# One decoder layer on one core: TensorE's feed at the start and at the two phase borders rearranged

## The chip, the cores and the metric

The kernel runs on one core of one Trainium2 chip. The metric is the device time of one execution in microseconds, as the median of several runs. The core's engines are TensorE (PE, matrix products; its weight loads are listed as PEld), VectorE (DVE), ScalarE (ACT), GpSimd (POOL) and SyncE (SP, which only issues transfers here). They run in parallel and wait for each other by semaphores.

## The reference, cut to what matters

One step of a decoder trunk with one layer, for 256 prompt tokens and 8 x 4 sample tokens (288 columns in all), model width 2048, feed-forward width 5632, all in float32:

```python
x = x + 0.5 * rmsnorm(swiglu(rmsnorm(x, g[0]), ffn1_w_in, ffn1_w_out), g[1])
m, sg, sh = hybrid_mixer(rmsnorm(x, g[2]), mix_w_in, ..., mix_w_out, s_gla, s_hgrn)
x = x + rmsnorm(m, g[3])
x = x + 0.5 * rmsnorm(swiglu(rmsnorm(x, g[4]), ffn2_w_in, ffn2_w_out), g[5])
```

`swiglu` is `(silu(gate) * up) @ w_out` with `gate, up` from `x @ w_in`. `hybrid_mixer` projects to queries, keys, values and gates, runs two groups of gated linear recurrences (GLA: 4 heads of 128 x 256 state; HGRN2: 8 heads of 128 x 128), each from a given state for the sample tokens, normalises the heads and projects back with `mix_w_out`. The outputs are the tokens and the new states.

## The kernel before

**Layout.** Model columns lie on the partitions, tokens along the free axis: `x[k]`, k = 0 to 15, are 16 tiles of 128 x 288. A float32 product is made of three products in the faster `fp32r` type: every weight `w` is split into `wh` (rounded, by ACT, L101) and `wl = w - wh` (by DVE, L102), and every `x` tile into `xh` (ACT, L272) and `xl` (DVE, L273). L556 to L558 are then `xh wh`, `xl wh` and `xh wl`, 128 x 288 results summed up in PSUM. So each tile of 128 x 128 weights costs PE three matmuls.

**Weights.** Class `Weights` (L40) moves all weights in units of 128 x 1024 (512 KB): `load` issues the transfer of a unit on SP's queue into one of three `raw` buffers, `pieces` splits it into one of four `wh`/`wl` pairs (two more pairs, the `extra` pool, exist around the phase borders). `ahead(most)` splits further units as long as `room()` finds a pair; `W.behind` may hold instructions behind which the next splits have to be issued (L111).

**Blocks.** `block` (L547) makes 512 output columns (four PSUM tiles) from the 16 x tiles: 8 units, two x tiles (k) each, for every k the four tiles f; after each unit it calls `W.ahead`. The last unit is taken tile by tile, each followed by its evacuation. `tick(k)` runs side work after a k. Five PSUM buffers serve the blocks.

**Phases.** Phase 1 is the first feed-forward net, phase 2 the mixer, phase 3 the second net. In each the first block (`gate1_0`, `qk0`, `gate2_0`) starts while the x tiles are still being made, and its results are used unnormalised; the second block (`up1_0`, `v0`, `up2_0`) carries the squares of x (`PreNorm.tick1`, L460), summed up in `acc`; `rstd` (L441) turns `acc` by an all-ones product on PE (`pre`, L445) into `rt`, which evacuations from then on multiply by.

**Borders.** `post_norm` (L521) ends a phase: `go` and `PreNorm.tick0` call `update(k)` for the 16 tiles (on DVE `y` times the norm, L529, and `x`, L530; then `xh` on ACT and `xl` on DVE). `Fill` lets PE begin the next phase with products of the old `x` (`old`) and of the unnormalised `y` (`new`) for four tiles. At the second border the code is the same.

**Start.** Transfers of x, gains and the first weights are issued from SP and ACT (L297 and after). x comes by token and is turned on PE (`x_turn`, L317). `WARM` transposes of the identity run ahead on PE. `row` (L560) makes the first three k in an order of its own; `second` (L358) turns and splits the second tile inside the first `row`.

**Side work on POOL.** `setup` (L893 and after, run from `pn.late`) fills masks and small operands of the mixer, `a32` (L911) among them. `load_state` of `block_scan` (L1293) loads the recurrent states of the first GLA heads (256 KB each, eight buffers), L1298.

**Order.** A planner orders each engine's instructions by a model of their times, in the order of the code where nothing else decides; `tc.issue_after(ins)` puts what follows behind `ins` on `ins`'s engine. Each engine then runs its list strictly in order, so an instruction that waits holds all behind it.

## Time and profile before

| | us |
|---|---|
| median of 3 runs (2259.80 to 2262.47) | 2261.17 |
| the profiled execution, its own time | 2261.81 |
| its span, first to last instruction | 2260.0 |
| PE busy | 2248.0 (99%) |
| DVE, ACT, POOL busy | 1362.2, 1005.1, 77.9 |
| data moved | 377.94 MB, mean 167 GB/s |

Part 1 of the page gives the busy time of each engine, with matmuls counted to their modelled end, so that short halts of PE do not show there. The view of the waits, for one engine, adds up who waited for whom. The chain of waits follows the end of the program back to what released each step. The view of stretches gives the busy time of each engine in a window, with the clock granted to TensorE (1.00 is 2.4 GHz, 0.50 is 1.2 GHz) and the rate of the transfers. Timelines list instructions in order of time: start, duration, engine, line, what is written from what, and in brackets the idle time before and what ended it.

### The profile page before, as it was taken

How to read it: one execution, taken by the hardware profiler on the slowest of the kernel's cores; microseconds unless marked ns; L12 is line 12 of the kernel's file. 1: busy time of each engine (PE TensorE's matmuls, PEld its weight loads, DVE VectorE, ACT ScalarE, POOL GpSimd, SP SyncE). 2: the span in 40 equal slices, each digit the busy share in tenths (PEclk: the TensorE clock that was granted, in tenths of full speed). 3: DMA queues.
4: the chain of work that ended last, by engine and by line, in shares of the span. 5: the costliest groups of instructions: out<-in, count | busy, mean ns of one | idle time of the engine just before them, and what ended most of it. 6: DMA issues, size and time to landing. Idle time of an engine off the chain costs nothing.

```text
span 2260.0 us, 41348 instructions
## 1 busy us (share of the span) xinstructions
PE 2248.0 (99%) x17075; PEld 2230.2 (99%) x17075; DVE 1362.2 (60%) x2167; ACT 1005.1 (44%) x1509; POOL 77.9 (3%) x143
## 2 busy tenths in 40 slices
PE   9999999999999999999999999999999999999998
PEld 9999999999999999999999999999999999999998
DVE  7545545555555568778788755844555455545545
ACT  5443333333334344545565644544333343333345
POOL 0000000000000003022110000100000000000000
PEclk9999999999999999999999999999999999999999
DMA  6555555555556555476565554555555555555553
GB/s 211 168 164 165 166 168 168 163 165 168 168 163 182 169 166 163 128 217 201 172 171 166 175 184 124 168 168 166 163 167 167 168 160 167 163 166 166 167 163 115
DMA packets 207378, 377.94 MB, mean 167 GB/s; under 512 B 15426, under 2 KB 41072, under 8 KB 207184
## 3 DMA queue, kind: packets, MB, share of 16 engines
q1 hardware_dynamic: 198736, 356.56, 52.9%
q0 software_dynamic: 5984, 17.97, 2.5%
q8 instruction: 135, 2.21, 0.4%
q10 hardware_dynamic: 2464, 0.70, 0.2%
q14 instruction: 59, 0.48, 0.1%
HBM read 363.39 MB, written 11.80 MB: 166 GB/s over the span
## 4 chain that ended last, share of the span: by engine, by line
PE 96%; DVE 2%; DMA 1%; ACT 1%; issue 1%; SPq 0%; DVEq 0%; ACTq 0%
PE gate L557 10%; PE gate L558 10%; PE gate L556 10%; PE out L557 8%; PE out L558 8%; PE out L556 8%; PE up L558 8%; PE up L556 8%; PE up L557 8%; PE mo L558 2%; PE mo L556 2%; PE mo L557 1%; PE hfq L556 1%; PE hfq L557 1%; PE hfq L558 1%; PE v L556 1%
## 5 line engine op out<-in xcount | busy, mean ns | idle before, releaser
L102 DVE TENSOR_TENSOR wl<-raw,wh 128x1024 fp32r<-128x1024 f32 (+1 forms) x674 | 822.0, 1220 | 647.1 <-ACT wh L101 644.6
L101 ACT ACTIVATE wh<-raw 128x1024 fp32r<-128x1024 f32 (+1 forms) x673 | 710.6, 1057 | 1057.5 <-PE gate L557 314.0
L556 PE MATMUL gate<-xh,wh 128*128 128x288 f32 x1660 | 488.8, 298 | 0.2 <-ACT xh L272 0.2
L557 PE MATMUL gate<-xl,wh 128*128 128x288 f32 x1660 | 488.7, 296 | 0.2
L558 PE MATMUL gate<-xh,wl 128*128 128x288 f32 x1660 | 488.6, 296 | 0.0
L557 PE MATMUL out<-hl,wh 128*128 128x288 f32 x1408 | 416.4, 296 | 0.0
L556 PE MATMUL out<-hh,wh 128*128 128x288 f32 x1408 | 415.8, 295 | 0.0
L558 PE MATMUL up<-xh,wl 128*128 128x288 f32 x1408 | 415.7, 295 | 0.0
L557 PE MATMUL up<-xl,wh 128*128 128x288 f32 x1408 | 415.5, 295 | 0.0
L558 PE MATMUL out<-hh,wl 128*128 128x288 f32 x1408 | 415.5, 295 | 0.0
L556 PE MATMUL up<-xh,wh 128*128 128x288 f32 x1408 | 415.1, 295 | 0.0
L557 PEld LDWEIGHTS gate<-xl,wh 128*128 128x128 f32 x1660 | 312.0, 188 | 1.5 <-DVE xl L273 1.0
L556 PEld LDWEIGHTS gate<-xh,wh 128*128 128x128 f32 x1660 | 311.1, 189 | 1.0 <-ACT xh L272 0.7
L558 PEld LDWEIGHTS gate<-xh,wl 128*128 128x128 f32 x1660 | 312.0, 188 | 0.0
L556 PEld LDWEIGHTS out<-hh,wh 128*128 128x128 f32 x1408 | 265.1, 188 | 0.0
L558 PEld LDWEIGHTS out<-hh,wl 128*128 128x128 f32 x1408 | 265.0, 188 | 0.0
L557 PEld LDWEIGHTS out<-hl,wh 128*128 128x128 f32 x1408 | 264.9, 188 | 0.0
L558 PEld LDWEIGHTS up<-xh,wl 128*128 128x128 f32 x1408 | 264.6, 188 | 0.1
L556 PEld LDWEIGHTS up<-xh,wh 128*128 128x128 f32 x1408 | 264.4, 188 | 0.1
L557 PEld LDWEIGHTS up<-xl,wh 128*128 128x128 f32 x1408 | 264.5, 188 | 0.1
L707 DVE TENSOR_TENSOR y<-out,y 128x288 f32<-128x288 f32 x287 | 121.0, 453 | 103.3 <-PE out L558 100.5
L556 PE MATMUL hfq<-xh,wh 128*128 128x288 f32 x256 | 78.1, 305 | 0.0
(383 smaller groups left out, 2404.3 us busy)
## 6 DMA issues: line engine op xcount, KB each, us to landing
raw<-in_ffn_w_in_dram SPq DMA_DIRECT2D x351, 512.0 KB, 3.7
raw<-in_ffn_w_out_dram SPq DMA_DIRECT2D x176, 512.0 KB, 3.7
raw<-in_mix_w_in_dram SPq DMA_DIRECT2D x64, 512.0 KB, 3.7
raw<-in_mix_w_in_dram SPq DMA_DIRECT2D x96, 256.0 KB, 3.4
raw<-in_mix_w_out_dram SPq DMA_DIRECT2D x32, 512.0 KB, 3.7
out_dram<-s POOLq DMA_DIRECT2D x32, 256.0 KB, 3.4
s<-in_state_gla_dram POOLq DMA_DIRECT2D x16, 256.0 KB, 4.6
s<-in_state_hgrn_dram POOLq DMA_DIRECT2D x16, 256.0 KB, 4.5
```

The costliest lines, as they stand in the source:

```text
L101: i1 = self.nc.scalar.activation(h[:, c], raw[:, c], AF.Copy).ins
L102: i2 = self.nc.vector.tensor_tensor(l[:, c], raw[:, c], h[:, c].bitcast(F32), op=ALU.subtract).ins
L556: yield lambda: PE.matmul(dst, w[0][:, c:c + P], parts[0], start=start, stop=False)
L557: yield lambda: PE.matmul(dst, w[0][:, c:c + P], parts[1], start=False, stop=False)
L558: yield lambda: PE.matmul(dst, w[1][:, c:c + P], parts[0], start=False, stop=stop)
L707: V.tensor_tensor(y[k], ps, y[k], op=ALU.add)
```

## The change

The calls of `ahead` hold `W.behind` until a pair of buffers is free. The blank parts of the x buffers are filled ahead of the loads; the second half of the first weight unit goes to SP's queue, behind the x columns 128 to 512 of the sample tokens; the identity's transposes on PE become matmuls on a blank tile, with one among the first x transposes and four behind them, and the products `xl wh` of the first k come ahead of the second tile's transposes. `tick0` puts the next splits behind the last tile's `xh` and `xl`; `tick1` makes its squares in four ticks instead of eight and `rstd` one tick later; the sum of the fill is put ahead of the splits after the first block, which no longer splits after its unit 6. `block` gets `head`: `v0` and `up2_0` take their first two units tile by tile (f outside, k inside). On POOL a copy from `k` after the block `qk0` (`gated`) precedes the state loads and the memset of `a32`.

```diff
@@ -108,7 +108,7 @@
         return held < (2 if more else HL_BUFS)
 
     def ahead(self, most=99):
-        if self.behind is not None:
+        if self.behind is not None and self.room():
             behind, self.behind = self.behind, None
             with ExitStack() as es:
                 for ins in behind:
@@ -287,39 +287,52 @@
         nc.sync.dma_start(xins[s][:, 0:2, c0 - s * 512:c1 - s * 512],
                           x_prompt[0, :, c0:c1].rearrange("(t p) c -> p t c", p=P))
 
+    def blank_sample(c0, c1):
+        s = c0 // 512
+        V.memset(xins[s][:, 2, c0 - s * 512:c1 - s * 512], 0.0)
+
     def load_sample(c0, c1):
         s = c0 // 512
-        V.memset(xins[s][:, 2, c0 - s * 512:c1 - s * 512], 0.0)
         nc.sync.dma_start(xins[s][0:TS, 2, c0 - s * 512:c1 - s * 512],
                           x_sample[:, :, c0:c1].rearrange("b t c -> (b t) c"))
 
-    unit = W.load_parts((S, S))
+    blank = ldp.tile([P, P], F32, name="blank", bufs=1)
+    V.memset(blank, 0.0)
+    for c0, c1 in ((0, P), (P, 512), (512, 1024), (1024, 1536), (1536, D)):
+        blank_sample(c0, c1)
+    unit = W.load_parts((S, nc.sync))
     S.dma_start(stage, norm_gains.rearrange("o g (k p) -> (o g k) p", p=P))
     load_prompt(0, P)
     next(unit)
     load_sample(0, P)
-    next(unit)
     load_prompt(P, 2 * P)
     load_sample(P, 4 * P)
+    next(unit)
     load_prompt(2 * P, 4 * P)
     for s in range(1, 3):
         W.load()
         load_prompt(s * 512, (s + 1) * 512)
         load_sample(s * 512, (s + 1) * 512)
     warm = auxtile("warm")
-    for _ in range(WARM):
-        last = PE.transpose(warm[:, 0:P], ident, ident).ins
+
+
+    def keep_warm(n):
+        for _ in range(n):
+            ins = PE.matmul(warm[:, 0:P // 2], blank, blank[:, 0:P // 2], start=True, stop=True).ins
+        return ins
+
     tp = auxtile("tp_prm")
-    with tc.issue_after(last):
-        PE.transpose(tp[:, 0:96], stage, ident[0:96, 0:96])
+    with tc.issue_after(keep_warm(WARM)):
+        first.last = PE.transpose(tp[:, 0:96], stage, ident[0:96, 0:96]).ins
     prm1 = V.tensor_copy(prm[:, 0:96], tp[:, 0:96]).ins
 
     def x_turn(k):
         s, c = k // 4, slice(k % 4 * P, (k % 4 + 1) * P)
         tp = auxtile(f"tp_x{k}")
         for t in range(2):
-            PE.transpose(tp[:, t * P:(t + 1) * P], xins[s][:, t, c], ident)
-        first.last = PE.transpose(tp[:, TP:TP + P], xins[s][:, 2, c], ident).ins
+            ins = PE.transpose(tp[:, t * P:(t + 1) * P], xins[s][:, t, c], ident).ins
+        with tc.issue_after(keep_warm(1) if k == 0 else ins):
+            first.last = PE.transpose(tp[:, TP:TP + P], xins[s][:, 2, c], ident).ins
         return tp[:, 0:T]
 
     def x_copy(k, tp):
@@ -346,11 +359,11 @@
 
     pieces = W.pieces(2)
     after((), lambda: next(pieces))
-    tps = [x_turn(0)]
+    with tc.issue_after(first.last):
+        tps = [x_turn(0)]
     after((), x_split, 0, tps[0])
     with tc.issue_after(first.last):
-        for _ in range(WARM // 4):
-            PE.transpose(warm[:, 0:P], ident, ident)
+        keep_warm(4)
     after((), lambda: next(pieces))
 
     made = []
@@ -456,13 +469,15 @@
         def tick0(self, k):
             if k + self.ahead < KT:
                 self.split = self.update(k + self.ahead)
+                if self.made is None and k + self.ahead == KT - 1:
+                    W.behind = self.split[:2]
 
         def tick1(self, k):
-            if k < 8:
+            if k < 4:
                 with tc.issue_after(self.split[0]), tc.issue_after(self.split[1]):
-                    for j in (2 * k, 2 * k + 1):
+                    for j in range(4 * k, 4 * k + 4):
                         sq_add(x[j], j)
-            if k == 9:
+            if k == 10:
                 ins = rstd(rt, (acc,), self.name)
 
                 behind = [G.memset(gate[:, 0:1], 0.0).ins, V.tensor_copy(gate[:, 1:2], epst).ins,
@@ -515,7 +530,7 @@
             V.tensor_tensor(self.sum, self.sum, self.scale[:, 0:T], op=ALU.mult)
 
         def total(self, ps):
-            V.tensor_tensor(self.sum, self.sum, ps, op=ALU.add)
+            W.behind = [V.tensor_tensor(self.sum, self.sum, ps, op=ALU.add).ins]
             return self.sum
 
     def post_norm(gcol, gnext, lasts, name, fill):
@@ -544,7 +559,8 @@
         return update
 
 
-    def block(name, nk, rhs, evac, width=512, tick=None, tail=1, hold=False, most=99, fill=None, made=None):
+    def block(name, nk, rhs, evac, width=512, tick=None, tail=1, hold=False, most=99, fill=None, made=None,
+              head=0):
 
         nf, per = width // P, 1024 // width
         nu = nk // per
@@ -561,11 +577,12 @@
 
             rows = [list(mm3(ps[f][:, 0:T], w, f, k, rhs(k), k == 0, False)) for f in range(nf)]
             made.extend(row[0]().ins for row in rows)
-            if k == 0:
-                after(made[-1:], second)
-                after((), lambda: (x_copy(1, tps[1]), x_copy(0, tps[0])))
-            with tc.issue_after(first.last if k == 0 else made[-1]):
-                made.extend(row[i]().ins for i in (1, 2) for row in rows)
+            for i in (1, 2):
+                with tc.issue_after(first.last if (k, i) == (0, 2) else made[-1]):
+                    made.extend(row[i]().ins for row in rows)
+                if (k, i) == (0, 1):
+                    after(made[-1:], second)
+                    after((), lambda: (x_copy(1, tps[1]), x_copy(0, tps[0])))
 
         def mm(w, f, k):
             if made is not None and k < 3:
@@ -579,14 +596,24 @@
 
         if fill:
             fill.products(lambda dst, k, parts, stop: mm3(dst, ws[k // per], 0, k, parts, k == 0, stop), ps[0][:, 0:T])
-        for u in range(nu - tail):
+        if head:
+            assert head * per == nf
+            first_ws = [W.next() for _ in range(head)]
+            for f in range(nf):
+                for k in range(nf):
+                    mm(first_ws[k // per], f, k)
+                if tick is not None:
+                    tick(f)
+            W.ahead(most)
+        for u in range(head, nu - tail):
             w = ws.pop(0) if ws else W.next()
             for k in range(u * per, (u + 1) * per):
                 for f in range(nf):
                     mm(w, f, k)
                 if tick is not None:
                     tick(k)
-            W.ahead(most)
+            if not fill or u < nu - tail - 1:
+                W.ahead(most)
             if fill and u == 5:
                 fill.scaled()
         ws = [W.next() for _ in range(tail)]
@@ -650,7 +677,7 @@
                     block(f"gate{tag}_{c}", KT, xrhs, ev_gate)
                 if final and c == 0:
                     last_pool()
-                block(f"up{tag}_{c}", KT, xrhs, ev_up, tick=pn.tick1 if c == 0 else None)
+                block(f"up{tag}_{c}", KT, xrhs, ev_up, tick=pn.tick1 if c == 0 else None, head=2 if c == 0 and fill else 0)
 
             lasts, zs = [], []
 
@@ -908,7 +935,8 @@
                     for i in range(4):
                         G.dma_start(aw[g][TS * i:TS * i + 16, 0:256], gla_up[0][:, 256 * g:256 * g + 256])
 
-                G.memset(a32[:, :, 16:TS], 0.0)
+                with tc.issue_after(gated[0]):
+                    G.memset(a32[:, :, 16:TS], 0.0)
                 V.tensor_tensor(a32[:, :, 0:16], araw, prm[:, 2 * KT:3 * KT].unsqueeze(2).broadcast_to([P, KT, 16]),
                                 op=ALU.mult)
                 G.memset(Dg, 0.0)
@@ -1295,7 +1323,8 @@
                     for _ in range(min(m, len(loads))):
                         a, b0 = loads.pop(0)
                         t = sp[0].tile([P, nb, dv], F32, name="s0", tag="s0", bufs=8)
-                        G.dma_start(t, s0[b0:b0 + nb, a].rearrange("b p v -> p b v"))
+                        with tc.issue_after(gated[0]):
+                            G.dma_start(t, s0[b0:b0 + nb, a].rearrange("b p v -> p b v"))
                         states[a, b0] = t
 
                 def blocks(t):
@@ -1561,7 +1590,7 @@
                             apart(1, 0)
                         yield
 
-            gens, later = [], []
+            gens, later, gated = [], [], []
 
             def tick(k=None):
 
@@ -1647,10 +1676,12 @@
                 block(f"qk{g}", KT, xrhs, ev_gla(d, g == 0), tick=tick if g else pn.tick0, most=99 if g else 1,
                       fill=None if g else border.fill)
                 if g == 0:
+
+                    gated.append(G.tensor_copy(gate[:, 0:1], d["k"][:, 1, 0:1]).ins)
                     scan_pool()
                 vt = vtiles(f"g{g}")
                 if g == 0:
-                    block("v0", KT, xrhs, ev_v(*vt), tick=pn.tick1)
+                    block("v0", KT, xrhs, ev_v(*vt), tick=pn.tick1, head=2)
                     lower_bounds()
                     a_lr()
                     gla_decay(d, g)
```

## Rows read from the trace of the kernel before

**Rows 1.** Page, part 1: busy time of each engine.

```profile
PE 2248.0 (99%) x17075; PEld 2230.2 (99%) x17075; DVE 1362.2 (60%) x2167; ACT 1005.1 (44%) x1509; POOL 77.9 (3%) x143
```

**Rows 2.** Stretches: length, busy (x instructions) by engine, granted clock, DMA share, GB/s.

```profile
100.00:200.00 100.00, 100.00 (x757) 100.00 (x756) 49.21 (x63) 43.40 (x60) 0.00 (x0) 1.00 0.54 163
```

**Rows 3.** PE's waits: us in total, times, longest.

```profile
PE qk L556 <- ACT xh L272: 1.8, 1, 1.8
...
PE pre L445 <- DVE acc L418: 1.1, 2, 0.6
...
PE gate L556 <- ACT xh L272: 0.2, 1, 0.2
```

**Rows 4.** Timeline of the first 30 us: start, duration, engine, line.

```profile
1.61 2.40 PE L311 MATMUL warm<-ident 128*128 128x128 f32 x10 [1.61 <-POOL epst L250]
...
5.39 1.33 PE L556 MATMUL gate<-xh,wh 128*128 128x288 f32 x4 [0.16 <-ACT xh L272]
...
6.77 0.63 ACT L101 ACTIVATE wh<-raw 128x512 fp32r<-128x512 f32 x1 [1.43 <-DMA raw<-in_ffn_w_in_dram]
...
7.97 0.50 ACT L272 ACTIVATE xh<-tp_x,prm 128x288 fp32r<-128x288 f32 x1 [0.57 <-PE tp_x L322]
...
10.14 1.25 PE L556 MATMUL gate<-xh,wh 128*128 128x288 f32 x4
```

**Rows 5.** Chain of waits, first 40 us: start, duration, step.

```profile
1.92 5.06 DMA xin<-in_x_prompt_dram
...
7.93 0.96 PE gate L557 x4
```

**Rows 6.** Timeline of PE, 880 to 890 us.

```profile
882.26 0.29 PE L558 MATMUL qk<-xh,wl 128*128 128x288 f32 x1
884.38 0.83 PE L556 MATMUL qk<-xh,wh 128*128 128x288 f32 x4 [1.83 <-ACT xh L272]
...
888.52 0.29 PE L558 MATMUL qk<-xh,wl 128*128 128x288 f32 x1
```

**Rows 7.** Stretches of 5 us at the first border.

```profile
875.00:880.00 5.00, 5.00 (x40) 5.00 (x39) 5.00 (x11) 2.03 (x3) 5.00 (x14) 1.00 0.94 313
...
885.00:890.00 5.00, 5.00 (x29) 5.00 (x28) 3.56 (x6) 1.98 (x5) 5.00 (x12) 0.66 0.68 210
```

**Rows 8.** Chain of waits of the whole span.

```profile
875.46 7.28 DMA raw<-in_mix_w_in_dram
...
915.87 2.08 PE a_lr L1608 x32
```

**Rows 9.** Timeline of ACT at the first border.

```profile
882.84 1.06 ACT L101 ACTIVATE wh<-raw 128x1024 fp32r<-128x1024 f32 x1 [4.44 <-DMA raw<-in_mix_w_in_dram]
```

**Rows 10.** Timeline of DVE at the first border.

```profile
880.54 0.94 DVE L530 SCALAR_TENSOR_TENSOR x<-y,hg,x 128x288 f32<-128x288 f32 x2
881.40 1.36 DVE L102 TENSOR_TENSOR wl<-raw,wh 128x1024 fp32r<-128x1024 f32 x1
...
890.34 0.82 DVE L1597 COPY k_g<-qk 128x288 f32<-128x288 f32 x2
...
913.51 0.42 DVE L963 TENSOR_TENSOR y<-v,rt 128x256 f32<-128x256 f32 x1 [0.25 <-PE v L558]
```

**Rows 11.** Page, part 6: transfers by issue, KB each, median us to landing.

```profile
raw<-in_mix_w_in_dram SPq DMA_DIRECT2D x64, 512.0 KB, 3.7
```

**Rows 12.** Timeline of POOL at the first border.

```profile
872.92 4.95 POOL L1298 DMA_DIRECT2D s<-in_state_gla_dram  x7 [12.42 <-PE qk L557]
...
889.82 0.20 POOL L924 CAST bmask<-bm 96x8 f32<-96x8 int32 x1
```

**Rows 13.** Timeline of ACT at the second border.

```profile
1419.87 1.06 ACT L101 ACTIVATE wh<-raw 128x1024 fp32r<-128x1024 f32 x1 [0.82 <-DMA raw<-in_ffn_w_in_dram]
```

**Rows 14.** Timeline of DVE at the second border.

```profile
1423.98 1.22 DVE L102 TENSOR_TENSOR wl<-raw,wh 128x1024 fp32r<-128x1024 f32 x1
```

**Rows 15.** Timeline of PE at the second border.

```profile
1426.76 0.29 PE L556 MATMUL up<-xh,wh 128*128 128x288 f32 x1
```

## The prediction

> **What bounds the kernel now.** I read part 1 of the page first: TensorE (PE) is busy for 2248.0 of 2260.0 us [rows 1], so what an edit can gain is time in which PE sits idle or runs slowly, and no more. Then the steady rate: the stretch from 100 to 200 us holds 757 matmuls in 100 us [rows 2], so one product (128 x 288) costs 0.132 us when PE is fed. Then the view of the waits, for PE alone: it names few of them, 1.8 us at `qk`, 1.1 us in two waits at `pre`, 0.2 us at `gate` [rows 3]. VectorE (DVE) and ScalarE (ACT) matter only where PE waits on them. Three places remain.
>
> *The start.* The first four products begin at 5.39 us [rows 4]. The next ones take 0.96 us for four, 0.24 us each [rows 5]; only after the group at 10.14 do they step at 0.132. That is the 1.2 GHz level against the 2.4 GHz one. (The view of the stretches prints a granted clock of 1.00 for the first ones; the product times decide.) The first four are over at about 6.35, and PE then waits for the transposes of the second tile: the chain runs through the load of those x columns, issued at 1.92 and landing 5.06 us later, at 6.98 [rows 5]. With the step from landing to start that is about 0.7 us.
>
> *The border from phase 1 to phase 2.* A product starts at 882.26, the next group only at 884.38, after 1.83 us without work [rows 6], and the granted clock of 885 to 890 reads 0.66 [rows 7]. From 882.26 to 888.52, where PE is at full clock again, twenty products start; at 0.132 us that is 2.64 us and it took 6.26, so 3.6 us are lost. Why is in the chain: a weight load took 7.28 us from issue to landing [rows 8], ACT's split `wh` waited 4.44 us for it until 882.84 [rows 9], and `xh` of the last two tiles, for which PE waited [rows 3], stood behind that split in ACT's order, although their `x` had been finished by 881.5 [rows 10]. Weight loads of this stage land in 3.7 us in the median [rows 11]. This one shared the DMA engines with seven state loads that POOL issued from 872.92 [rows 12]; together they moved 313 GB/s in 875 to 880 [rows 7].
>
> *The border from phase 2 to phase 3* is the control: the same block and splits, no state load. ACT's split again stands ahead of the last `xh`, but its load holds it for 0.82 us only, to 1419.87 [rows 13], and the view of PE's waits has no more than 0.2 us for all of `gate` [rows 3]. So the order alone does no harm; the order with a slow load does.
>
> *Both second blocks* halt PE at `pre`, which waits for the last addition to `acc`: two waits, the longer 0.6 us [rows 3].
>
> **The change, part by part** (against the profiled execution, 2261.81 us, with a span of 2260.0; the median of the runs is 2261.17, so 0.6 is taken off at the end).
>
> (1) State loads later, gated on a POOL copy of `k`. The eight loads leave 873 to 878 and go after `k`'s evacuation, which ends at 891.2 before [rows 10] and 3.6 us earlier after. The load issued at 875.46 then lands in about 3.7 us, near 879.2, where ACT is idle; `xh` follows `x` at about 881.5 and PE finds it at 882.39. Together with (2) this gives back the whole **3.6 us**. Each part covers for the other, so they are counted once.
>
> (2) Last x tiles ahead of splits. `W.behind` pins the next split behind the last `xh` and `xl`. On DVE this exchanges the `wl` at 881.40 (1.36 us) with the two `xl` [rows 10]. No term of its own; it pushes the splits of the second block's first two units to the edge, see (4).
>
> (3) Squares four per tick, `rstd` one tick later. The sums can end earlier and are asked for 1.6 us later (12 products by 0.132 us), against waits of 0.6 us at most. Gain **1.1 us**. What is late next is `rt`, which the evacuation of the second block needs and which comes up to 1.0 us later against PE than before (one tick, less the wait). Before, that evacuation at 913.51 waited for PE's products [rows 10], so `rt` was not the last to come; and a later evacuation holds PE only when the fifth PSUM buffer is used up.
>
> (4) Second block tile by tile (`head`). The same products in another order. It relaxes the PSUM: the second tile is wanted after twelve products (1.6 us), not three (0.4 us). It tightens the weights: the second unit is wanted after six (0.8 us), not 24 (3.2 us). By DVE's durations: `xl` done at about 882.4 (two `x` end at 881.5 [rows 10]), then two `wl` at 1.22 [rows 14] and the fill's scaling, about 0.5, so the second unit is ready near 885.5; the first block ends at 882.39 + 24 x 0.132 = 885.6, and that unit's `wl` is wanted 1.1 us later. At the other border `wl` of the second unit ends at 1425.2 [rows 14], and the second block's run of products begins at 1426.76 [rows 15]. The margin is 1 us or less. Bounds of its cost: 0 to one `wl` (1.22 us) at each border, and no gain, since no PSUM wait shows there [rows 3]. I take **0.3 us lost** over both, as the margin is positive but thin.
>
> (5) The start. Warm-up matmuls on a blank tile need one DVE memset instead of POOL's identity, so they begin about 0.4 us before the old 1.61 [rows 4]; they end before the first products can run (5.39), so they cost nothing. The `xl` products come ahead of the second tile's transposes and fill the 0.7 us. The second half of weight unit 0 leaves ACT's queue for SP's, behind the second x columns; SP's later x and weight loads move back by one issue (about 0.5 us). Upper bound: the 0.7 us, two later slow groups and most of the third, 2.8 x (0.96 - 0.53) = 1.2, and two sets of three transposes at some 0.1 us too much each, 0.6: 2.5 us. Lower bound: the 0.7 us alone. A cap lies between: the second `k` needs the other half of the split, which began when its load landed (6.77, 0.63 us), and `xh` of the second tile (0.50 us) behind it [rows 4]. With landing at 6.8 to 7.2, that is 8.3, against 10.14 before [rows 4]: 1.8, and its own slow group gives up to 0.4. I take **1.9 us**. It stays gained if the weights keep pace: the view of the waits has none of PE's for a split there [rows 3], and the next loads wait for buffers that the splits free, which follow PE. So they move up with it; if they don't, nothing of this term is left, which the range takes in.
>
> A rule of the Trainium skill speaks against this part. TensorE: Matmul & The Clock Gate (Part 4: PE-mode transpose) says that transposes do not raise the clock as products do. The trace cannot part this from the gap: ten transposes from 1.61 on, and the gap at 6.4, were followed by slow products [rows 4, 5]. By that rule, the transposes of gains and x that stay among the warm-up could still hold the clock down; only the 0.7 us would then be gained.
>
> (6) At nothing: POOL's set-up (12 us, from the end of the state loads at 877.87 to 890.0 [rows 12]) now stands behind the gate at 887.6 and eight issues of 0.71 us, so it ends near 905; its first reader on PE is `a_lr` at 915.87 [rows 8], about 912 after. Cover 7 us; if it were gone, each us late would halt PE by one.
>
> Sum: 3.6 + 1.1 + 1.9 - 0.3 = 6.3. 2261.8 - 6.3 = 2255.5, less 0.6 for the median: **2255.0 us**.
>
> **Rivals.**
> - *Clock no earlier.* The start gains 0.7 only: 5.1 in all, 2256.1. For it: all that precedes the first products at 5.39 includes transposes, now as before. Against: the gap goes, and at the border it was products that stood before the return to 2.4 GHz [rows 6].
> - *The collision moves.* The state loads now meet the weight loads of `v0` (from 887.5), the 3.6 us come back there: gain 2.7, 2258.5. For it: 2 MB in 6 us, as before. Against: two split units stand ahead there (24 products each, 3.2 us), and a split has until they are used up, so 3.6 us more of landing is just covered; and no `xh` stands behind a split any more.
> - *Slower: the head starves.* Place: the first eight products of each second block. It decides from the point where the second unit's `wl` ends later than these, by so much that the clock falls as it did at 884 [rows 6]. Price: the 3.6 us of that row plus one `wl`, 4.8 us at each border; border 1 nets 1.2 worse, border 2 4.8, less 3.0 for start and `pre`: 3.0 slower, 2264.2. For it: margins of 1 us and splits pinned behind the last tiles. Against: it needs a delay of over 1 us to begin, and near 2 us of idle PE for the clock to fall as it did; only one `wl` is close to late.
> - *It doesn't do what it says.* The planner lets the unpinned second split ahead of `xh` again, or POOL's order changes little: 2.1 of 3.6 stay lost, 2257.0.
>
> **How the numbers follow.** Forecast 0.62 (2253.5 to 2256.5), clock no earlier 0.15, collision 0.10, no effect 0.05, head 0.08. Range 2252.8 to 2259.0: below, all bounds at their best (7.2 us) and 1.2 us for the spread of the runs (2259.8 to 2262.47); above, the collision. A measurement of this kernel can tell about 0.2% (4.5 us, 2256.65) from no change; the second case straddles that line, and of the head's 0.08 I give 0.05 to a price half as much again, which passes the line on the other side (2265.7). Faster 0.70, same 0.25, slower 0.05.
>
> **What would show it.** No PE wait at `qk` and a granted clock of 1.00 through 885 to 890; POOL's state loads after `k`'s copies; no PE wait at `pre`; four products in 0.53 us before 8 us; the second `k` of the first block near 8.3. Wrong if PE waits inside the first twelve products of a second block, or if weight loads in `v0` hold ACT.

## The result, and the profile of the changed kernel

The change makes the kernel slower. Median before 2260.26 us (13 runs, 2258.52 to 2262.47), after 2265.43 us (13 runs, 2263.96 to 2266.69); ratio 1.0022, 95% interval 1.0013 to 1.003, so 5.2 us. The forecast was 2255.0 with a range of 2252.8 to 2259.0. One profile, that of the first run of the gate alone, is of a disturbed execution and is not read.

The profiled execution of the changed kernel has a span of 2264.1 us (before 2260.0). In what follows a *shift* is the start of a PE instruction less the start of the same instruction in the kernel before, taken from the two traces:

| PE instruction | before | after | shift |
|---|---|---|---|
| first product | 5.39 | 8.22 | +2.83 |
| second k | 10.14 | 12.30 | +2.16 |
| `qk0`, first product | 855.88 | 857.76 | +1.88 |
| `v0`, its 25th product | 892.09 | 890.49 | -1.60 |
| `a_lr` (behind `v0`) | 915.80 | 919.03 | +3.23 |
| `mo`, first product | 1293.35 | 1297.78 | +4.43 |
| last norm | 2247.20 | 2251.06 | +3.86 |

So the start loses where it was to gain, the first border gains 3.5 us, `v0` loses 4.8, the mixer 1.2, and the second border gains 0.6.

The start, from PE's timeline of the changed kernel (start, duration, engine, line, as in [rows 4]):

```profile
1.21 4.53 PE L321 MATMUL warm<-blank 128*128 128x64 f32 x20 [1.21 <-DVE blank L300]
5.53 0.37 PE L326 MATMUL tp_prm<-ident,stage 96*128 96x96 f32 x1
...
6.65 1.81 PE L321 MATMUL warm<-blank 128*128 128x64 f32 x8
8.22 1.31 PE L572 MATMUL gate<-xh,wh 128*128 128x288 f32 x4
9.32 1.16 PE L573 MATMUL gate<-xl,wh 128*128 128x288 f32 x4
...
12.30 0.77 PE L572 MATMUL gate<-xh,wh 128*128 128x288 f32 x4
```

PE has no gap behind 1.21, and the trouble is what fills it: the ten warm-up matmuls stand as twenty instructions of 0.23 us, 4.53 us where the ten transposes took 2.40 [rows 4], and the gains' transpose behind them starts at 5.53. PEld, which loads the weights of each, is busy for 4.34 us with the same twenty; which of the two sets the pace is not shown. The four later ones hold the first products to 8.22. Although PE was busy from 1.21 on, it is at 2.4 GHz only from about 12 us.

The first border and `v0`, by stretches (start and end, length, busy time of PE, PEld, DVE, ACT, POOL with their instructions, granted clock, DMA share, GB/s), to hold against [rows 7]:

```profile
885.00:890.00 5.00, 5.00 (x40) 5.00 (x39) 5.00 (x9) 2.96 (x6) 0.92 (x1) 1.00 0.55 162
895.00:900.00 5.00, 5.00 (x40) 5.00 (x39) 3.90 (x6) 1.84 (x4) 5.00 (x18) 1.00 0.99 355
900.00:905.00 5.00, 4.99 (x38) 4.76 (x36) 2.51 (x4) 2.24 (x5) 4.79 (x13) 1.00 1.01 327
905.00:910.00 5.00, 1.11 (x6) 1.03 (x7) 3.44 (x5) 3.39 (x6) 2.90 (x7) 0.99 0.69 208
910.00:915.00 5.00, 5.00 (x29) 5.00 (x28) 5.00 (x12) 3.08 (x7) 0.00 (x0) 0.67 0.67 146
```

At 885 PE is whole, as forecast. Twenty microseconds later the picture of [rows 7] stands again: 355 GB/s, PE without work, a granted clock of 0.67. POOL's, ACT's and PE's lines (as in [rows 9, 12, 6]) and one piece of the chain of waits (as in [rows 8]) tell why:

```profile
890.09 5.71 POOL L1327 DMA_DIRECT2D s<-in_state_gla_dram  x8
```
```profile
895.74 9.12 DMA raw<-in_mix_w_in_dram
```
```profile
896.15 1.06 ACT L101 ACTIVATE wh<-raw 128x1024 fp32r<-128x1024 f32 x1 [1.03 <-DMA raw<-in_mix_w_in_dram]
897.12 0.76 ACT L427 ACTIVATE sq<-x 128x288 f32<-128x288 f32 x2
900.96 1.06 ACT L101 ACTIVATE wh<-raw 128x1024 fp32r<-128x1024 f32 x1 [3.08 <-DMA raw<-in_mix_w_in_dram]
...
904.93 1.06 ACT L101 ACTIVATE wh<-raw 128x1024 fp32r<-128x1024 f32 x1 [0.81 <-DMA raw<-in_mix_w_in_dram]
905.90 0.76 ACT L427 ACTIVATE sq<-x 128x288 f32<-128x288 f32 x2
```
```profile
908.89 0.72 PE L458 MATMUL pre<-acc,onesD 128*128 128x288 f32 x2 [3.90 <-DVE acc L431]
```

The eight state loads run beside weight loads of which one needs 9.12 us to land; ACT's splits wait for them; the squares (L427) stand behind those splits; the sum of the squares is late, and PE, which needs it for `pre`, stands for 3.9 us; soon after, its products take 0.24 us each, the 1.2 GHz level, until 913. The view of PE's waits has, in place of the `qk` of [rows 3]:

```profile
PE pre L458 <- DVE acc L431: 3.9, 1, 3.9
PE sc L1436 <- DVE Qv L1391: 2.0, 2, 1.4
```

The wait at `pre` is no accident of one execution: it is 2.9 to 4.4 us in the five runs below that keep the gate and the four squares per tick and change the warm-up alone.

### The profile page after: what moved, and what is told of

Same layout as the page of the kernel before. It is cut to its first block, busy times and chain, and to the rows that moved or that the text cites. A ratio compares the mean times of both kernels' runs of the same rounds, so it can differ in the third digit from the quotient of the medians.

```text
span 2264.1 us, 41388 instructions
## 1 busy us (share of the span) xinstructions
PE 2250.4 (99%) x17093; PEld 2233.6 (99%) x17093; DVE 1362.8 (60%) x2168; ACT 1004.6 (44%) x1509; POOL 77.3 (3%) x144
## 4 chain that ended last, share of the span: by engine, by line
PE 96%; DVE 2%; DMA 1%; ACT 0%; issue 0%; SPq 0%; DVEq 0%; ACTq 0%
PE gate L572 10%; PE gate L574 10%; PE gate L573 10%; PE out L573 8%; PE up L574 8%; PE up L572 8%; PE out L574 8%; PE up L573 8%; PE out L572 8%; PE mo L574 2%; PE mo L572 1%; PE mo L573 1%; PE hfq L572 1%; PE hfq L573 1%; PE hfq L574 1%; DMA raw<-in_mix_w_in_dram 1%
```

## Experiments at the first border and in v0

In the table below each median (us) stands beside that of the kernel before in the same series. An interval that reaches 1 does not by itself tell a run from the kernel before.

| run | median | before | ratio (95%) |
|---|---|---|---|
| states after `rt` | 2260.11 | 2260.52 | 0.9997 (0.9988 to 1.0006) |
| states early | 2259.64 | 2260.52 | 0.9996 (0.9986 to 1.0005) |
| gate alone | 2257.94 | 2259.84 | 0.9992 (0.9983 to 1.0001) |
| gate alone, again | 2258.23 | 2260.01 | 0.9992 (0.9981 to 1.0002) |

**State loads behind `rt`.**

```diff
-                        with tc.issue_after(gated[0]):
+                        with tc.issue_after(gated[-1]):
                             G.dma_start(t, s0[b0:b0 + nb, a].rearrange("b p v -> p b v"))
@@ after block v0
+                    gated.append(G.tensor_copy(gate[:, 0:1], rt[:, 0:1]).ins)
```

> The changed kernel with its state loads moved once more: on POOL they now stand behind a copy of rt, which the evacuation of the block v0 waits for, instead of behind the copy of k. All of the computation is included. Theory A (the state loads collide with the weight loads of v0: one took 9.12 us to land, ACT's splits waited 1.03, 3.08 and 0.81 us for such, the squares stood behind them on ACT, and PE waited 3.9 us at pre and then ran at half clock): no wait at pre, no stretch below clock 0.95 from 900 to 915, about 4.8 us off: 2260.6, unless the states are then late for the scan. Theory B (the squares four per tick make ACT and DVE too late by themselves, whatever the loads do): the wait at pre stays at 3 to 4 us and the end at 2265.4. Theory C (the collision moves on): pre is free, but the loads hold the weights of the next block, and 2 to 4 us come back behind 915: 2263 to 2265.

Measured: 2260.11. PE's waits at `pre` shrink to

```profile
PE pre L458 <- DVE acc L431: 0.2, 1, 0.2
```

and the shift through `v0` goes from -2.42 to -2.79, where the changed kernel goes from -1.60 to +3.23. Theory A. The squares four per tick are on time when no load is late, so theory B falls; the clock is 1.00 in every stretch from 900 to 915, and behind 915 nothing comes back but the wait in the mixer that other runs have too (below), so theory C falls.

**State loads where they were, order of the splits kept.**

```diff
-                        with tc.issue_after(gated[0]):
-                            G.dma_start(t, s0[b0:b0 + nb, a].rearrange("b p v -> p b v"))
+                        G.dma_start(t, s0[b0:b0 + nb, a].rearrange("b p v -> p b v"))
```

> The changed kernel with the state loads where the kernel before has them, ahead of the first border (only the memset of a32 stays behind the copy of k); the splits still stand behind the last x tiles. All of the computation is included. Theory A (the order of the splits alone is enough at the first border, since nothing that PE needs at once stands behind the late weight load): no wait at qk, no wait at pre, the whole 4.8 us back: 2260.6. Theory B (a weight load that lands 7 us after its issue holds PE by itself, whatever stands behind it): PE idles 2 to 4 us between 884 and 890 instead of at 905 and the end is at 2263 to 2265. The prediction counted the two parts once, each as the cover of the other; this run shows whether that holds.

Measured: 2259.64. The view of PE's waits has neither `qk` nor `pre`. The stretch 880 to 885, with the loads back in it, and ACT's split of the late unit:

```profile
880.00:885.00 5.00, 5.00 (x40) 4.95 (x39) 4.67 (x11) 2.38 (x5) 0.00 (x0) 1.00 0.99 351
```
```profile
886.74 1.06 ACT L101 ACTIVATE wh<-raw 128x1024 fp32r<-128x1024 f32 x1 [1.02 <-DMA raw<-in_mix_w_in_dram]
```

The transfers are as dense as ever (351 GB/s) and a split waits for one, but PE does not: `xh` is ahead of the split now. The border's gain is the same with the gate and without (shift +1.88 to -1.60 with, +1.84 to -1.65 without), and 3.5 us again in the later runs without `head` (-1.98 to -5.48) and with squares two per tick (-2.56 to -6.05). So the order alone does it, theory A, and the gate on the state loads earns nothing beside it; it costs the 5.9 us between the ratios 1.0022 and 0.9996, whose intervals are apart.

**The gate alone, in the kernel before.** The edit is the change's lines on `gated` only (L911, L1298, L1649 of before); two of them:

```diff
+                    gated.append(G.tensor_copy(gate[:, 0:1], d["k"][:, 1, 0:1]).ins)
@@ load_state
+                        with tc.issue_after(gated[0]):
```

> The kernel before with one part of the change alone: the copy of k on POOL, with the state loads and the memset of a32 behind it. Start, squares and the order of the splits are as before, all of the computation is included. Theory A (the state loads cost where they meet weight loads with something of PE's behind the split; moving them moves that cost): the 3.6 us of the first border come back there (no wait at qk, clock near 1.00 from 885 to 890), PE then waits 2 to 4 us at pre with a fall of the clock near 910, and the end is 0 to 1.5 us above the kernel before: 2260.5 to 2262. Theory B (the loss at pre comes from the squares taken four per tick, not from the loads): no wait at pre beyond the 1.1 us of before and the end at 2256.9. Theory C (a gate alone leaves the splits ahead of xh, and the wait at qk stays at 1 us or more for another reason): the first border returns 2 us at most.

> The same kernel as the run of before with the gate alone, looked at once more, since the first look's profile is of a disturbed execution and shows nothing of the borders. The median of that run, 2257.94 against 2259.84 of before, is a gain of 1.9 where theory A had said 0 to 1.5 slower and theory B 3.6 faster. Theory A' (the 3.6 of the first border come back and the loads collide in v0 here too, but squares two per tick leave less of it for PE): no wait at qk, 1.5 to 3 us at pre, span about 2258. Theory B' (no collision that PE feels without the squares four per tick; the first border returns about 2): no wait at pre above 1.1, a wait of 1 us or more left at qk. The start is that of the kernel before: the first groups 0.96 each and the fast products from 10 to 11 us on, if the clock rises there in every execution; if it differs by execution, as the run with the old start suggests (0.79 for the first four at 5.70), this look may show either.

Measured: 2257.94 and 2258.23, 1.9 and 1.8 ahead of before; each interval just reaches 1. In the second run's trace the shift goes from -2.73 to -6.30 over the border (3.6 gained), then to -3.48 over `v0` (2.8 lost), with

```profile
PE pre L445 <- DVE acc L418: 2.4, 2, 1.9
```
```profile
900.00:905.00 5.00, 3.49 (x17) 3.42 (x18) 3.93 (x5) 4.04 (x8) 4.10 (x10) 0.77 0.85 178
```

A': the collision moves with squares two per tick as well, and takes 2.8 us instead of 4.8. That the difference is due to the squares alone is argued, not shown: the splits differ in order too. By trace the net gain is 0.8; the medians say 1.8 to 1.9. Theory A's bound (no gain) is not borne out.

## Experiments at the start

| run | warm-up | median | before | ratio (95%) |
|---|---|---|---|---|
| half | five float32, 64 columns, zeros | 2262.41 | 2260.52 | 1.0009 (1.0 to 1.0019) |
| half, ones | the same with ones | 2262.74 | 2259.30 | 1.0015 (1.0004 to 1.0026) |
| wide | two float32, 288 columns, zeros | 2262.82 | 2259.30 | 1.0017 (1.0006 to 1.0028) |
| fp32r, ones | ten, 288 columns | 2262.41 | 2260.52 | 1.0008 (0.9999 to 1.0017) |
| fp32r, zeros | ten, 288 columns | 2262.80 | 2259.84 | 1.0012 (1.0002 to 1.0022) |
| six fp32r, states early | six, 288 columns, ones | 2258.92 | 2259.84 | 0.9993 (0.9984 to 1.0002) |
| old start, states early | ten transposes | 2256.59 | 2259.84 | 0.9988 (0.9979 to 0.9997) |
| the same, new row order | ten transposes | 2256.60 | 2260.01 | 0.9984 (0.9975 to 0.9993) |

**Half the warm-up.**

```diff
-WARM = 10
+WARM = 5
-        keep_warm(4)
+        keep_warm(1)
```

> The changed kernel with half as many warm-up products: five instead of ten ahead of the gains' transpose, one instead of four ahead of the first products. Everything else as in the changed kernel, all of the computation included. Theory A (the start was lost to the length of the warm-up: its ten float32 matmuls stand in the trace as twenty of 0.23 us, 4.53 us in all from 1.21, and the gains' transpose stands behind them at 5.53 though the gains had landed at 3.4): the gains' transpose at about 3.5, the first product at 5.3 to 5.6 instead of 8.22, the second k near 9 to 10 instead of 12.30, and 2 to 3 us off the end: 2262.4 to 2263.4 against the 2265.4 of the changed kernel. Theory B (the start is set by the loads: SP's transfers of x and weights moved back): the first product moves, but the second k and the weights of the first block hold PE, and the end gains less than 1 us: 2264.5 to 2265.5. For the clock: if the warm-up matmuls raise it, fewer of them leave the first products slow for longer; if the first real products do, it rises about 4 us after the first of them, as in both kernels.

Measured: 2262.41, 3.0 less than the changed kernel. PE's timeline:

```profile
3.42 0.39 PE L326 MATMUL tp_prm<-ident,stage 96*128 96x96 f32 x1
...
5.55 1.33 PE L572 MATMUL gate<-xh,wh 128*128 128x288 f32 x4 [0.27 <-ACT xh L272]
...
9.73 0.83 PE L572 MATMUL gate<-xh,wh 128*128 128x288 f32 x4
```

Each time is as theory A had it. The products at 2.4 GHz begin with the second k, as in the changed kernel.

**Another kind of warm-up.** Four kernels set the clock at the first products beside the kind of warm-up. The first differs from the changed kernel so, the second has 0.0 for 1.0; the third keeps float32 and takes 288 columns (WARM = 2); the fourth is the half warm-up with ones.

```diff
-    V.memset(blank, 0.0)
+    V.memset(blank, 1.0)
+    ones_r = ldp.tile([P, T], F32R, name="ones_r", bufs=1)
+    V.tensor_copy(ones_r, blank)
-            ins = PE.matmul(warm[:, 0:P // 2], blank, blank[:, 0:P // 2], start=True, stop=True).ins
+            ins = PE.matmul(warm[:, 0:T], ones_r[:, 0:P], ones_r, start=True, stop=True).ins
-        keep_warm(4)
+        keep_warm(2)
```

> The changed kernel with a warm-up of another kind: ones instead of zeros, in fp32r, 288 columns, the shape and type of the real products; ten ahead of the gains' transpose, one among the transposes of the first tile, two behind. All of the computation is included. It takes about as long as the warm-up of the run with half as many float32 ones (0.24 us each at the low level, 2.4 us for ten), so the two differ in what the warm-up consists of. Theory A (only products like the real ones raise the clock; the 64-column products of zeros don't): the products already step at 0.132 from the first or second group on, that is four in about 0.55 to 0.7 us before 8 us, and the end is 1 to 2 us ahead of the run with half as many: about 2261 to 2262. Theory B (the kind makes no difference; the transposes between them or the first real products decide): the first groups take 0.96 each in both, the clock rises at the same time within 0.5 us, and the two ends are within 0.5 us of each other, 2262.4 to 2263.4.

> The run with ten fp32r warm-up products of 288 columns, with zeros instead of ones in both operands; nothing else differs, all of the computation is included. Theory A (the form of the products raises the clock, not what they hold): the first four products take about 0.80, as with ones, and the following groups 0.72 and 0.77. Theory B (products of zeros don't raise it, which would also explain the changed kernel, whose warm-up multiplies zeros): the first groups take 1.1 to 1.3 and 0.96 each, and the second k begins near 10 instead of 8.69.

> The changed kernel with a warm-up of zeros in float32 as it has, but 288 columns wide instead of 64 and fewer: two products ahead of the gains' transpose, one among the first transposes, one behind. All of the computation is included. It parts the two features in which the fp32r warm-up (zeros and ones alike: the first products at 2.4 GHz, 0.80 for four) differs from the changed kernel's. Theory A (the width): the clock is up within the first two groups of products, four in 0.8 or less. Theory B (the type: float32 products do not raise it here, of whatever width): the first groups take 0.96 to 1.16 each and the fast ones begin some 4 us after the first real product, as in the changed kernel (8.22 and 12.3) and with half the warm-up (5.55 and 9.7). The duration of one of these is not in any trace so far; at four times the columns, 0.9 to 1.0 us for both its instructions, the gains' transpose stands at 3.4 to 4.0 and the first product at 5.5 to 6.5.

> The run with half the float32 warm-up, 64 columns, with ones instead of zeros; all of the computation is included. Theory A (neither the data nor the count matters for these): the clock rises as there, at 9.7, some 4 us after the first product at 5.55, and the second k begins at 9.7. Theory B (with data other than zero, float32 products raise it too): four products in 0.8 or less before 8 us, the second k at 8.3 to 8.7.

Measured, the first four products in PE's timeline, in this order:

```profile
6.22 0.80 PE L574 MATMUL gate<-xh,wh 128*128 128x288 f32 x4 [0.33 <-ACT xh L272]
```
```profile
6.42 0.80 PE L574 MATMUL gate<-xh,wh 128*128 128x288 f32 x4 [0.32 <-ACT xh L272]
```
```profile
6.25 0.80 PE L572 MATMUL gate<-xh,wh 128*128 128x288 f32 x4
```
```profile
5.46 1.33 PE L572 MATMUL gate<-xh,wh 128*128 128x288 f32 x4 [0.27 <-ACT xh L272]
```

After the three warm-ups of 288 columns, float32 or fp32r, zeros or ones, the first products run at 2.4 GHz (0.80 for four); after the two of 64 columns, zeros or ones, at 1.2 GHz (1.33), as in the changed kernel and the two runs with its start and other state loads (1.31). In these executions the level goes with the width of the warm-up products and not with data or type. Each kernel has one profiled execution, though, and with the old start the level at the same products differs from execution to execution (below): what decides is not shown. At the end little of it is left: the ratios 1.0008 to 1.0017 overlap with the half warm-up's 1.0009. In the fp32r run the shift is -1.66 at the 25th product and -0.84 at the end of the first block; the theory's 1 to 2 us more at the end did not come.

**The start of the kernel before.** Hunks of the change on the start and `row` are left out, the state loads are early.

> The changed kernel with state loads where the kernel before has them and with the start of the kernel before (ten transposes as the warm-up, loads and rows in the old order); the parts at the borders are kept. All of the computation is included. It differs from the run with early state loads by the start alone. Theory A (the new start costs 1.84 us at the end of the first block in that run, and PE has no slack behind it): 2259.64 - 1.8 = 2257.8, that is 2.5 us ahead of the kernel before. Theory B (part of the start's loss is taken up later, where PE waits for something else): 2258.5 to 2259.5.

Measured: 2256.59. Against states early (2259.64) that is 3.1 us by the medians and 2.4 when each is set against its own before: the new start costs that much in the end, theory A, and more than its 1.8. No PE wait at `qk` or `pre` is left in its trace.

**Row order alone**, on top of the last one: the change's hunk in `row`.

> The run with the old start with one part of the new start alone: the products xl wh of the first k ahead of the second tile's transposes. Warm-up and loads are as in the kernel before, all of the computation is included. Theory A (the prediction's lower bound: PE waits 0.74 us for the second x columns, the four products fill it): the four xl products begin right behind the first four, near 6.4, no wait for the x columns, and the second k begins 0.5 to 0.7 us earlier: the end at 2255.9 to 2256.2. Theory B (the second k waits for the second half of the first weights, landed at 6.95 there, and its own transposes, which now come later): it begins no earlier and the end stays at 2256.3 to 2257. The clock is a question of its own: if it rises at another moment from execution to execution with this warm-up, single looks at the four kernels of this call with the old warm-up differ by up to 2 us at the second k.

Measured: 2256.60. The `xl` products fill the wait for the second x columns, as the prediction had it:

```profile
5.40 1.10 PE L559 MATMUL gate<-xh,wh 128*128 128x288 f32 x4 [0.16 <-ACT xh L272]
6.34 0.75 PE L560 MATMUL gate<-xl,wh 128*128 128x288 f32 x4
...
8.34 0.77 PE L559 MATMUL gate<-xh,wh 128*128 128x288 f32 x4
```

The second k begins at 8.34 against 8.95, but the shift at the end of the first block is -1.53 against -2.03: given back, as far as two executions can tell. The medians are equal and the ratios overlap: theory A was right on the second k, theory B on the end. Both kernels beat the kernel before and the changed one.

These two, the gate alone (its second run) and the two runs of the next section have the warm-up of the kernel before, and in the five profiled executions PE is at 2.4 GHz from some moment between 5.4 and 7.6 us on. Its timeline in the old start and in the gate alone:

```profile
5.70 0.79 PE L559 MATMUL gate<-xh,wh 128*128 128x288 f32 x4 [0.16 <-ACT xh L272]
```
```profile
5.41 0.80 PE L556 MATMUL gate<-xh,wh 128*128 128x288 f32 x4 [0.24 <-ACT xh L272]
```

The same four took 1.10 to 1.33 in the other three, and 1.33 in the execution that the prediction read [rows 4], where the clock rose behind 10.14. That execution was a late one: its time, 2261.81, is 1.6 above the median of 13.

**Six fp32r warm-up products**, states early.

```diff
-WARM = 10
+WARM = 6
-        keep_warm(2)
+        keep_warm(6)
```

> The changed kernel with state loads where the kernel before has them and with a warm-up of ones in fp32r, 288 columns: six ahead of the gains' transpose, one among the first transposes, six behind them. All of the computation is included. Theory A (the warm-up then ends near 3.4, when the gains land; the clock is up before the first products, as with ten of these; and what is gained up to the second k is partly given back in the first block, 1.66 to 0.84 us in the run with ten): first product at 5.5 to 5.8, four in under 0.85 us, second k at 8 to 8.7, the end of the first block 0.8 to 1.2 us ahead of the kernel before, and the end at 2256.5 to 2257.2, some 0.8 to 1.2 ahead of the run with the old start. Theory B (six are too few, the first groups take 0.96 each): the start is as with half the float32 ones and the end at 2257.5 to 2258.5, no better than with the old start.

Measured: 2258.92, 2.3 behind the old start. SP's queue has the prompt's second x columns ahead of the first sample columns, as in the run with ten, where these landed at 5.13; here they landed at 6.00. In PE's timeline PE stands for them, and the first products run at 1.2 GHz:

```profile
6.05 0.48 PE L337 MATMUL tp_x<-ident,xin 128*128 128x128 f32 x1 [1.42 <-DMA xin<-in_x_sample_dram]
...
7.77 1.16 PE L574 MATMUL gate<-xh,wh 128*128 128x288 f32 x4
```

Neither theory had that. Whether six are enough without the pause was not tried, and why the load came 0.9 later stays open.

This execution also shows that early state loads are no sure cure at `pre`. A weight load issued at 880.03, while they were under way, took 8.33 us; ACT's split waited for it, and the squares stood behind that split:

```profile
880.03 8.33 DMA raw<-in_mix_w_in_dram
```
```profile
888.47 1.06 ACT L101 ACTIVATE wh<-raw 128x1024 fp32r<-128x1024 f32 x1 [3.26 <-DMA raw<-in_mix_w_in_dram]
889.43 0.43 ACT L429 ACTIVATE acc<-x 128x288 f32<-128x288 f32 x1
```
```profile
PE pre L460 <- DVE acc L433: 1.2, 1, 1.2
```

Of four executions with early state loads and the change's order, squares and `head`, three have no PE wait at `pre` and this one has 1.2 us. Against the old start it loses 2.9 us before `qk0` and 1.3 over `v0` by trace.

## Experiments on the second blocks

Both start from the kernel with the old start and early states (2256.59, ratio 0.9988).

**Without `head`** (both `head=2` taken out).

> The run with the old start (early state loads, the order of the splits and the squares of the change) without the part that begins second blocks tile by tile: both second blocks take k outside and f inside again. All of the computation is included. Theory A (as predicted, that part moves only what is already free): 2256.0 to 2257.2 against 2256.59, no PE wait inside the first products of v0 or up2_0 in either. Theory B (it costs up to 1.2 us at each border by late weights): 0.5 to 2.4 us faster without it. Theory C (it gains, since a PSUM tile of the first block is not yet evacuated when the second block wants it): 0.4 to 1.2 us slower without it, with PE waiting for an evacuation near 883.

Measured: 2258.62 against 2260.01 of before, ratio 0.9995 (0.9986 to 1.0004): 2.0 us slower than with it by the medians, 1.6 by the ratios. The intervals of the two ratios overlap, so the size is uncertain; the traces bear out the sign. Its waits, in the view of PE's waits:

```profile
PE zp L1629 <- DVE y L1623: 0.9, 1, 0.9
PE pre L445 <- DVE acc L418: 0.7, 1, 0.7
```

Slower, as theory C had it and by more than its 1.2, but not by its mechanism: no wait for a PSUM tile stands near 883. By the code, `head` also calls the splits once behind the first two units instead of after each of them. From 883 to 891.3 ACT's timeline has four splits and five squares in the run without it, three splits and six squares, with two more begun, in the run with it. So with it the squares end earlier, `pre` starts 1.8 us earlier (901.13 against 902.94), and so comes `rt`, by which the `y` that `zp` waits for is multiplied: the shift at `zp` is -6.06 with `head` and -4.38 without. That the calls do this and not the order of the products was not tried apart.

**Squares two per tick**, `rstd` at its old tick.

```diff
-            if k < 4:
+            if k < 8:
-                    for j in range(4 * k, 4 * k + 4):
+                    for j in (2 * k, 2 * k + 1):
-            if k == 10:
+            if k == 9:
```

> The run with the old start with squares two per tick and rstd at its old tick; early state loads, order of the splits and the second blocks tile by tile are kept. All of the computation is included. Theory A (the prediction's step: 0.6 + 0.5 = 1.1 us were lost at the two waits at pre): the two waits at pre come back, 0.4 to 0.7 each, and the end is about 1.1 us later, 2257.2 to 2258. Theory B (with the borders shorter and the order of the splits changed, pre is no longer late): within 0.4 us of 2256.59, no wait at pre.

Measured: 2258.61 against 2260.01, ratio 0.9995 (0.9986 to 1.0004): 2.0 us slower than with four per tick by the medians, 1.6 by the ratios, with intervals that overlap here too. In the view of PE's waits:

```profile
PE pre L445 <- DVE acc L418: 2.0, 2, 1.3
```

The two waits are back, larger than the 1.1 of [rows 3]: theory A, with more than its 1.1.

## Why the prediction was wrong, step by step

- **(1) and (2), 3.6 us: right at the border.** It gave 3.5 (shift +1.88 to -1.60), and each part gives it alone: the gate 3.6 (-2.73 to -6.30), the order 3.5. They were rightly counted once. What failed is the rest of step (1): it moved eight transfers and priced what they leave, not what they enter.
- **The rival "the collision moves", given 0.10: this is what happened at `v0`.** The step that failed is the sentence against it, that no `xh` stands behind a split any more and a split has until two units are used up. True, and yet PE waited, because the *squares* stand behind splits in ACT's order and PE needs their sum at `pre`. The price was small too: 3.6 in the text, 4.8 measured (-1.60 to +3.23), as loads took up to 9.12 us and three splits in a row waited (1.03, 3.08 and 0.81 us). The run with the loads behind `rt` takes all of it away, and so does the run with early loads.
- **(3), 1.1 us: right where no load is late.** With the old start and early states the shift falls by 0.69 over `v0` and by 0.61 at the second border (-4.93 to -5.54), 1.3 in all; with squares two per tick it rises at both. It needs step (4) beside it: without `head` nothing is gained over `v0` (-5.48 to -5.43). In the changed kernel only the second border shows it: 0.57 (+4.43 to +3.86) against the 0.5 forecast. "What is late next is `rt`" named the wrong thing there: PE waited for `acc`.
- **(4), 0.3 lost: wrong in sign.** No product of a second block waited for weights; without `head` the kernel is 1.6 to 2.0 us slower, by intervals that overlap, and `pre` and `zp` are later by trace. The step looked at the products' order and PSUM, and left out that `head` also moves the calls of the splits and with them the squares.
- **(5), 1.9 gained: the largest miss.** The change lost 2.2 at the second k and 1.7 at the end of the first block against the execution shown, and 3.3 to 4.4 against the other executions of the old warm-up (shift -1.5 to -2.7 there in five, +1.7 in the changed kernel). The sentence that failed is "they end before the first products can run (5.39), so they cost nothing": the term was left at zero without a duration, though no row showed a float32 matmul of 64 columns. It measured 0.45 us each instead of the transposes' 0.24, so 2.1 us more for ten, and the four later ones took 1.8 us where two transposes had taken 0.6. Half the warm-up gave 3.0 back, and the old start 2.4 to 3.1. The 1.2 us for "later slow groups" were a loss of the execution that was read, and much smaller in the five others.
- **The rival "clock no earlier"** was near: the clock came no earlier in the changed kernel. Its reason was not the one: with the same transposes of gains and x among them, the warm-ups of 288 columns were followed by products at 2.4 GHz. The Trainium skill, TensorE: Matmul & The Clock Gate (Part 4: PE-mode transpose), says that transposes do not raise the clock as products do. By that rule the kernel before could not have been at 2.4 GHz at its first products; the runs disagree, since after ten transposes four products took 0.79 and 0.80 us in two executions and the clock was up by 7.6 us in three more. The same page (Part 1: The HAM clock gate) says that the number of slow matmuls at the beginning of a kernel varies from run to run, and with that these runs agree: 5.41 to behind 10.14 for one start.
- **(6): right.** POOL's set-up ended near 908, not 905, and `a_lr` (919.03) was not held by it.
- **The mixer's 1.2 us** were foreseen by no step. PE waits at `sc` for 0.6 us in the kernel before and in five of the runs, and for 1.4 to 2.0 in the changed kernel and eight others, with every kind of edit among both. No part of the change goes with it; what sets it stays open.

Sum, against the shown execution: start +1.9, border -3.5, `v0` +4.8, mixer +1.2, second border -0.6, which is +3.8, for the +3.86 at the last norm and +4.1 in the span. The medians are 5.2 apart: the execution shown was 1.6 above its median, the changed kernel's 0.5 above its own. That the 1.6 belong to the start is likely from the five other starts, not shown.

## What to carry to other kernels

When transfers are moved off a place where they collide, list every engine's queue at the place where they go: not only what the waiting instruction's own consumer needs, but all that stands behind it in its engine's order, down to the next thing that PE waits for. Changing who stands behind the late load was enough at the border, and moving the load beside that cost more than it gave; a load that is late enough still reached the next thing that PE waits for in one execution. A warm-up is on the path as soon as something that PE must do stands behind it: give it a duration from a row, or bound it, and never zero; and before a loss of the first microseconds is put into a sum, see whether it is in more than one execution.

## What the runs showed of the hardware

- A float32 matmul stands in the trace as two instructions: 0.45 us for both with 64 columns, ahead of the rise of the clock, where a 128-column transpose takes 0.24. Two of 288 columns took 2.29 us at the start of the kernel.
- In the changed kernel PE ran 64-column float32 products of zeros and transposes without a gap from 1.21 on, and its real products were at 1.2 GHz from 8.22 to about 12 us. With 288-column ones of the same type and data in their place the real products were at 2.4 GHz from the first, at 6.25. One execution each.
- With ten transposes as the warm-up the real products reached 2.4 GHz between 5.4 and 7.6 us in five executions, and only behind 10.14 in a sixth.
- A 512 KB weight load lands in 3.7 us [rows 11], in up to 9.12 (changed kernel, 327 to 355 GB/s) beside eight 256 KB loads from POOL's queue, and in 7.28 before [rows 8].
